# Two transformer blocks on one core: other duration estimates for side work, NSA compression in column quarters, 512-column feed-forward tails and memory values, small weights loaded first

## Chip, core and metric

The kernel runs on one core of a Trainium2 chip, as one program. The metric is the time of one execution in microseconds; lower is better. TensorE (PE) multiplies matrices, VectorE (DVE), ScalarE (ACT) and GpSimd (POOL) work on elements, SyncE (SP) issues most of the DMAs.

## What is computed

Two blocks of two layers each, on a sequence of 256 rows of 1024 elements. The first block's layer is a mixer (an LRU, "forgetting" attention with 8 heads, and retention with 4 heads), cross attention to a memory of 256 rows, and a gated feed-forward. The second block's layer is a feed-forward, a mixer of three attentions (NSA with a compressed, a selected and a window branch; stick-breaking; sliding window), and a second feed-forward. Cut to what the change touches:

```python
def swiglu(h, w_gate, w_up, w_down):              # six times in all
    return (jax.nn.silu(h @ w_gate) * (h @ w_up)) @ w_down

def memory_cross_attention(h, mem_n, w_q, w_k, w_v, w_o):
    k = (mem_n @ w_k).reshape(bsz, m, CROSS_HEADS, CROSS_HEAD_DIM)
    v = (mem_n @ w_v).reshape(bsz, m, CROSS_HEADS, CROSS_HEAD_DIM)
    ...

def compress(t, w1, w2):                           # in nsa_attention, for keys and for values
    blocks = t[:, cmp_idx] + cmp_pos[:, None, :]   # 15 overlapping blocks of 32 rows, 2 groups
    blocks = blocks.transpose(0, 3, 1, 2, 4).reshape(B, G, n_cmp, CMP_LEN * Dh)
    return jax.nn.silu(blocks @ w1) @ w2           # w1: 2048 x 256, w2: 256 x 64
```

## The kernel before

**Big products.** Every large matrix product is made of three FP32R products (hi x hi, hi x lo, lo x hi) of operands split into two parts. Weights come from HBM as raw chunks of 1 MB (class `Weights`, three raw buffers); ScalarE casts a piece to `whi`, VectorE subtracts to get `wlo`, up to six pieces ahead of TensorE. Activations are kept transposed and split (`thi`, `tlo`; `mhi`, `mlo` for the memory). Products gather in PSUM tiles `acc`, two of them in a ring. A raw chunk is freed, and the next load issued on SP, when its last piece is split. Feed-forward weights are taken in column blocks of 512 and one tail of 256: the gate's block, then the up block (`ffn`, `plan_ffn`). `gate_done` applies silu on ScalarE, `up_done` multiplies on VectorE.

**Side work.** Attention, the LRU, retention, the norms and the NSA compression are Python generators handed to `side()`. At fixed points between the big products the writer calls `pump()`. There, class `Pace` keeps an estimated clock for each engine while the program is written: each instruction adds an estimated duration, a tile's estimated time of being ready is kept, and a step of a side generator is put into the instruction streams once its inputs are estimated ready (0.3 us of slack) and a bank of the two `aux` PSUM tiles is free. Where the writer needs a result that isn't there yet, `finish()` or `pump(force=True)` puts the missing steps in one behind the other, with no big products between. The order in which instructions stand in each engine's stream is fixed by this at build time; on the chip an engine waits where an input is late. Small products write `aux`, `o0` and `o1`. All instructions are recorded by one helper, so the trace gives line 150 for nearly everything; groups are told apart by tile names.

**Names.** `sc`, `pt`, `fv`, `fkT`, `fqT`, `fT`: forgetting attention. `rot`, `rqkT`, `rvg`, `cv`, `bd`: retention and its rotary step (`h`: the LRU's output or a norm's row). `cqT`: cross attention. `kvout`: the memory's keys and values on their way to HBM (`fill_steps`). In the second mixer (`mixer2`): `rs`, `wkT`, `wqT`, `wv` sliding window; `rn`, `kT`, `qT`, `vsw` the selected and window branches of NSA, in eight units (transposes of `rn`, scores `kT,qT`, softmax, values `rn,vsw`); `kc`, `kcb`, `scmp`, `pc` the compressed branch; `w`, `hh`, `hv` its second weights and hidden rows.

**NSA compression.** `compress_blocks` lays out the blocks, splits them in two parts (`t`), and `compress_mm` multiplies them with the split weight: 30 output rows, 256 columns, three products per 128 rows of the weight, 96 per layer, between the branch gate's big products (`compress_mm` is called between weight pieces as planned by `plan_mixer2`). `compress_attention` turns the 30 rows by four transposes and loads the second weights and masks just before it uses them.

Of the kernel before, what the change touches and what calls it, by code (L numbers as in the profile page):

```python
# [48 lines left out]
class Pace:  # L49
# [3 lines left out]
    FIXED = {"vector": (0.065, 1.045e-3), "scalar": (0.075, 0.86e-3), "gpsimd": (0.13, 2.15e-3)}  # L53
# [3 lines left out]
    def __init__(self, nc):  # L57
# [3 lines left out]
        self.loads = 0.0  # L61
        for name in ("tensor", "vector", "scalar", "gpsimd", "sync"):
            self.at[name] = 0.0
            setattr(self, name, Paced(self, name, getattr(nc, name)))
# [22 lines left out]
    def op(self, name, op, args, kwargs):  # L87
# [15 lines left out]
        elif name == "tensor":  # L103
            moving = aps[2] if op == "matmul" else aps[0]
            rate = 1 if moving.dtype == F32R else 2 if op == "transpose" else 4
            self.products = start + max(0.027, size(moving) * rate / 2400.0) + 0.004
            done = self.products + 0.1
        else:
            fixed, each = self.FIXED[name]
            n = max(size(a) for a in aps)  # L110
            if kwargs.get("op") == ALU.pow:
                fixed, each = 0.3, 0.165
# [5 lines left out]
            self.at[name] = max(start, self.at[name]) + (fixed + each * n) + (0.09 if kwargs.get("accum_out") is not None else 0.0)  # L118
            done = self.at[name] + 0.1
# [35 lines left out]
class Weights:  # L155
# [10 lines left out]
    def plan(self, ap, c0, c1, k0, k1, a_chunk, a_piece, split=True, gain=None, halves=0):  # L166
# [4 lines left out]
        for k in range(k0, k1, a_chunk):  # L171
# [6 lines left out]
            self.chunks.append((parts, a, b))  # L178
            for j in range(0, a, a_piece):
                n = min(a_piece, a - j)  # L180
                self.pieces.append([ci, j, n, b, split, j + n >= a, None, list(range(k + j, k + j + n)), gain])
# [7 lines left out]
    def _load(self):  # L189
# [5 lines left out]
        for ps, ap in parts:  # L195
            self.nc.sync.dma_start(v[ps], ap)
# [72 lines left out]
def tile_two_blocks(ctx, tc, I, out):  # L269
# [52 lines left out]
    def mm(ps, a, b, start, stop):  # L322
        nc.tensor.matmul(ps, a, b, start=start, stop=stop)

# [11 lines left out]
    def pump(force=False):  # L336
# [33 lines left out]
    def two_aux():  # L370

        while max([nc.idle(a) for a in auxs[-2:]], default=0.0) > nc.products + 0.3:
# [31 lines left out]
    def pair_scores(q, k):  # L404

        pss = aux(), aux()
        for c, qs, ks in ((slice(0, P), slice(0, P), slice(0, P)), (slice(P, 384), slice(P, S), slice(0, S))):
            for u in (0, 1):
                mm(pss[u][:, c], q[HALF[u], qs], k[HALF[u], ks], start=True, stop=True)
        return pss  # L410

    def pair_scores_T(q, k):

        pss = aux(), aux()
        for c, ks, qs in ((slice(0, S), slice(0, P), slice(0, S)), (slice(S, 384), slice(P, S), slice(P, S))):
            for u in (0, 1):
                mm(pss[u][:, c], k[HALF[u], ks], q[HALF[u], qs], start=True, stop=True)
# [20 lines left out]
    def pair_pv(dst, ws, vs, start=True, stop=True):  # L438

        for kt, (c0, c1, q0) in enumerate(((0, S, 0), (S, 384, P))):  # L440
            for u in (0, 1):
                mm(dst[HALF[u], q0:S], vs[u][:, kt, :], ws[u][:, c0:c1], start=start and kt == 0, stop=stop and kt == 1)
# [330 lines left out]
    def plan_ffn(g, u, d, gain):  # L773
        for c0, c1 in FBLOCKS:
            for w in (g, u):
# [1261 lines left out]
```

## Time and profile before

| what | us |
|---|---|
| median of three runs (lowest, highest) | 2108.08 (2105.86, 2108.32) |
| the profiled execution | 2107.61 |
| its span in the trace | 2105.8 |
| TensorE busy | 2053.1 |
| VectorE busy | 1276.0 |
| ScalarE busy | 1120.7 |

The profiled execution lies between the three runs. TensorE's busy time overstates its work somewhat, because consecutive products overlap in the trace and their ends are modelled; the distance from start to start is the better measure of what one costs. In the views below "x" is a count, and what stands in square brackets or behind the bar is the idle time before an instruction and what ended it. PEclk is TensorE's granted clock as a share of full speed.

### The profile page before, as it was taken

The page shows a single profiled execution, that of the slowest core. Times are in us where ns is not written, and L with a number is a line of the kernel's source. Part 1 is how long each engine was busy: PE and PEld are TensorE (multiplying, and loading weights), DVE is VectorE, ACT ScalarE, POOL GpSimd, SP SyncE. Part 2 cuts the span into 40 slices and gives each one's busy share as a digit, 9 for nine tenths or more (in the row PEclk, how much of TensorE's full clock was granted, in tenths as well). Part 3 has the DMA queues.
Part 4 walks back from the last instruction along what each step waited for, and adds up shares of the span by engine and source line. Part 5 has one row for each costly group of instructions (what it writes and reads, how often), then busy time and mean ns, then how long its engine had stood idle before and what let it go on. Part 6 is the DMA issues. An engine that isn't in the chain of part 4 may idle for free.

```text
span 2105.8 us, 28507 instructions
## 1 busy us (share of the span) xinstructions
PE 2053.1 (97%) x10982; PEld 1717.3 (82%) x10982; DVE 1276.0 (61%) x2187; ACT 1120.7 (53%) x1910; POOL 84.7 (4%) x110
## 2 busy tenths in 40 slices
PE   7999999999899999999999999999999999999999
PEld 6889888888797788788888767888888887768887
DVE  6766566556664755655467666664655567756553
ACT  5556566455465654555355655554555456446552
POOL 0210000002100000000001000000000001000000
PEclk9999999999999999999999999999999999999999
DMA  7555565654465565555646544555555547545553
GB/s 244 182 194 190 186 212 180 212 178 158 148 225 175 182 198 191 172 187 180 210 145 207 169 140 158 193 176 193 180 196 194 162 151 230 144 132 183 179 197 103
DMA packets 204583, 380.86 MB, mean 181 GB/s; under 512 B 14160, under 2 KB 78464, under 8 KB 204448
## 3 DMA queue, kind: packets, MB, share of 16 engines
q1 hardware_dynamic: 192928, 366.46, 53.1%
q10 hardware_dynamic: 11520, 12.59, 2.0%
q8 instruction: 86, 1.41, 0.3%
q14 instruction: 49, 0.40, 0.1%
HBM read 372.03 MB, written 6.99 MB: 180 GB/s over the span
## 4 chain that ended last, share of the span: by engine, by line
PE 83%; DVE 6%; ACT 4%; DMA 4%; issue 2%; POOL 0%; SPq 0%; ACTq 0%; DVEq 0%; POOLq 0%
PE acc L150 74%; PE aux L150 6%; DVE wlo L150 3%; PE o L150 3%; ACT whi L150 1%; DMA nb<-cdram 1%; DMA raw<-in_w_in_dram 1%; DMA w<-in_nsa_cmp_k_w_dram 1%; ACT rn L150 1%; ACT thi L150 1%; DMA kvd<-kvout 0%; SPq L150 0%; DVE t L150 0%; DVE h L150 0%; DMA mem<-in_mem_dram 0%
## 5 line engine op out<-in xcount | busy, mean ns | idle before, releaser
L150 PE MATMUL acc<-whi,thi 128*128 128x512 f32 (+2 forms) x1856 | 716.2, 386 | 2.3 <-ACT thi L150 1.4
L150 PE MATMUL acc<-whi,tlo 128*128 128x512 f32 (+2 forms) x1856 | 699.9, 377 | 2.5 <-DVE tlo L150 2.4
L150 PE MATMUL acc<-wlo,thi 128*128 128x512 f32 (+2 forms) x1856 | 699.3, 377 | 3.1 <-DVE wlo L150 2.8
L150 DVE TENSOR_TENSOR wlo<-raw,whi 128x1024 fp32r<-128x1024 f32 (+1 forms) x386 | 463.0, 1210 | 310.1 <-ACT whi L150 308.3
L150 ACT CAST whi<-raw 128x1024 fp32r<-128x1024 f32 (+1 forms) x386 | 393.7, 1037 | 243.9 <-PE acc L150 219.9
L150 DVE SCALAR_TENSOR_TENSOR wlo<-raw,prm,whi 128x512 fp32r<-128x512 f32 (+1 forms) x640 | 398.5, 680 | 173.8 <-ACT whi L150 173.6
L150 ACT ACTIVATE whi<-raw,prm 128x512 fp32r<-128x512 f32 (+1 forms) x640 | 379.9, 663 | 90.2 <-PE acc L150 86.7
L150 PEld LDWEIGHTS acc<-whi,thi 128*128 128x128 f32 x1856 | 350.3, 189 | 72.4 <-issue 9.3
L150 PEld LDWEIGHTS acc<-whi,tlo 128*128 128x128 f32 x1856 | 349.9, 189 | 70.3 <-DVE tlo L150 6.4
L150 PEld LDWEIGHTS acc<-wlo,thi 128*128 128x128 f32 x1856 | 350.5, 189 | 64.4 <-DVE wlo L150 6.1
L150 PE MATMUL acc<-whi,ahi 128*128 128x512 f32 x528 | 206.9, 392 | 0.0
L150 PE MATMUL acc<-whi,alo 128*128 128x512 f32 x528 | 205.7, 389 | 0.0
L150 PE MATMUL acc<-wlo,ahi 128*128 128x512 f32 x528 | 205.6, 389 | 0.0
L150 PEld LDWEIGHTS acc<-whi,alo 128*128 128x128 f32 x528 | 99.1, 188 | 20.8
L150 PEld LDWEIGHTS acc<-whi,ahi 128*128 128x128 f32 x528 | 99.2, 188 | 19.9
L150 PEld LDWEIGHTS acc<-wlo,ahi 128*128 128x128 f32 x528 | 99.2, 188 | 19.9
L150 POOL TENSOR_TENSOR r<-v,mhalf 128x1 f32<-128x1 f32 (+3 forms) x46 | 48.1, 1047 | 1593.9 <-DVE v L150 1591.9
L150 PE MATMUL acc<-thi,whi 128*128 128x256 f32 x384 | 111.9, 291 | 0.0
L150 PE MATMUL acc<-tlo,whi 128*128 128x256 f32 x384 | 108.6, 283 | 0.0
L150 PE MATMUL acc<-thi,wlo 128*128 128x256 f32 x384 | 108.5, 283 | 0.0
L150 DVE SCALAR_TENSOR_TENSOR silu<-acc,r,silu 128x512 f32<-128x512 f32 (+1 forms) x72 | 47.5, 702 | 100.4 <-PE acc L150 100.4
L150 ACT CAST ahi<-aux 128x512 fp32r<-128x512 f32 (+1 forms) x72 | 39.8, 553 | 121.9 <-PE aux L150 121.7
(301 smaller groups left out, 1946.9 us busy)
## 6 DMA issues: line engine op xcount, KB each, us to landing
raw<-in_w_in_dram SPq DMA_DIRECT2D x65, 1024.0 KB, 5.1
raw<-in_ffn_w_gate_dram SPq DMA_DIRECT2D x44, 1024.0 KB, 5.1
raw<-in_ffn_w_up_dram SPq DMA_DIRECT2D x44, 1024.0 KB, 5.1
raw<-in_ffn_w_down_dram SPq DMA_DIRECT2D x44, 1024.0 KB, 4.9
raw<-in_w_gate_dram SPq DMA_DIRECT2D x22, 1024.0 KB, 5.0
raw<-in_w_up_dram SPq DMA_DIRECT2D x22, 1024.0 KB, 5.1
raw<-in_w_down_dram SPq DMA_DIRECT2D x22, 1024.0 KB, 4.8
raw<-in_w_out_dram SPq DMA_DIRECT2D x16, 1024.0 KB, 5.0
```

The lines of the kernel that those rows point to most:

```text
L150: return f(*args, **kwargs)
```

## The change

Five edits in one. (1) The estimates of `Pace` are other numbers, mostly longer, and the 0.3 us of slack in `pump` and `two_aux` is gone; the second of two products in opposite halves of the array counts as 7 ns. (2) The compression uses unsplit fp32 blocks and raw weights: four products of 32 output rows and 256 columns stand side by side, each in its own quarter of the array's columns, 32 per layer; the four partial sums are added by a product with `sel` (the identity folded four times), which takes the place of the transposes. The raw chunk is freed when TensorE is done with it. (3) The feed-forward tails of gate and up stand side by side as one block of 512 columns; silu and the product both follow its end. (4) The memory's value weights are taken in 512-column blocks, and `kvout` is written once per pair. (5) `load_small` issues the DMAs of the compression's second weights and masks when `compress_blocks` begins. Also: `xs` has one buffer, the sliding window waits for `blocks` where it waited for the split blocks, and the forgetting attention waits for a flag that its decay rows are on their way to HBM.

```diff
-    FIXED = {"vector": (0.065, 1.045e-3), "scalar": (0.075, 0.86e-3), "gpsimd": (0.13, 2.15e-3)}
+    FIXED = {"vector": (0.15, 1.06e-3), "scalar": (0.14, 0.89e-3), "gpsimd": (0.25, 3.3e-3)}
...
-            rate = 1 if moving.dtype == F32R else 2 if op == "transpose" else 4
-            self.products = start + max(0.027, size(moving) * rate / 2400.0) + 0.004
-            done = self.products + 0.1
+            main = moving.dtype == F32R
+            if op == "transpose":
+                took = 0.109
+            elif self.beside:
+                took = 0.007
+            elif main:
+                took = (size(moving) + 32) / 2400.0
+            else:
+                took = max(0.224, size(moving) * 4 / 2400.0)
+            self.products = start + took + (0.09 if main != self.main else 0.0)
+            self.main = main
+            done = self.products + 0.25
...
-            due = [i for i in ready if i[1] <= nc.products + 0.3 and aux_free() <= nc.products + 0.3]
+            due = [i for i in ready if i[1] <= nc.products and aux_free() <= nc.products]
...
-                W.plan(I[f"nsa_cmp_{kv}_w1_2"][l], 0, 256, 8 * k, 8 * k + 8, 8, 4)
+                W.plan(I[f"nsa_cmp_{kv}_w1_2"][l], 0, 256, 8 * k, 8 * k + 8, 8, 4, split=False)
...
-                            mm3(a[:30, k * S : k * S + S], bh[:, k, kt, :], bl[:, k, kt, :], hi[:, j, :], lo[:, j, :], kt == 0, kt == 15)
+                            mm(a[32 * j : 32 * j + 32, k * S : k * S + S], blocks[:, k, kt, :], w[:, j, :], i == 0, i == 3, beside=j > 0)
...
-                        turn(ps[:, (2 * k + b) * 30 : (2 * k + b + 1) * 30], raw[:, k * S + b * P : k * S + (b + 1) * P], ident[:30, :30])
+                        mm(ps[:, (2 * k + b) * 30 : (2 * k + b + 1) * 30], raw[:, k * S + b * P : k * S + (b + 1) * P], sel[:, :30], start=True, stop=True)
...
-            for w in (g, u):
-                W.plan(w, c0, c1, 0, 8, 4 if c1 - c0 == 512 else 8, 2 if c1 - c0 == 512 else 4, gain=gain)
+            if c1 - c0 == 512:
+                for w in (g, u):
+                    W.plan(w, c0, c1, 0, 8, 4, 2, gain=gain)
+            else:
+                W.plan(g, c0, c1, 0, 8, 4, 2, gain=gain, beside=u)
...
+                    if n < 512:
+                        hold["n"] = n
+                        gate_done(a)
...
+            W.plan(I["w_cv"][l], c // 2 * 512, c // 2 * 512 + 512, 4 * (c % 2), 4 * (c % 2) + 4, 4, 2)
...
+                        if kind == "v":
+                            mm3(a[:, b * 512 : b * 512 + 512], MT.hi[:, kt, bs], MT.lo[:, kt, bs], hi[:, j, :], lo[:, j, :], kt == 0, kt == 7)
...
-                    xs = mp.tile([P, 16, 32], F32, tag="xs", name=nm("xs"))
+                    xs = mp.tile([P, 16, 32], F32, tag="xs", name=nm("xs"), bufs=1)
...
             def compress_blocks():
+                load_small()
```

How TensorE's stream moves is shown at two places of the second mixer in layer 0. The first is where the sliding window, the compressed branch and one NSA unit stand. Before, on PE, with twelve or six big products (`acc`) between the steps:

```order
L150 MATMUL aux_10735<-w_856_10666,hh_10645 30x64 x2
L150 MATMUL aux_10735<-w_857_10667,hv_862_10679 128x64 x2
L150 MATMUL o_10655<-rs_10725,wv_9544 64x256
...
L150 MATMUL acc_10569<-whi_10535,thi_9111 128x512
...
L150 MATMUL aux_10780<-ident_90,kc_10743 128x30
L150 MATMUL acc_10784<-whi_10553,thi_9111 128x512
...
L150 MATMUL aux_10809<-kcb_10782,qT_9546 128x30 x8
L150 MATMUL acc_10784<-whi_10605,thi_9111 128x512
...
L150 MATMUL aux_10835<-ident_90,rn_10695 128x128 x3
```

With the change, on PE, the same steps:

```order
L163 MATMUL aux_10356<-w_781_9645,hh_10289 30x64 x2
L163 MATMUL aux_10356<-w_782_9646,hv_854_10315 128x64 x2
L163 MATMUL o_10378<-rs_10327,wv_9147 64x256
...
L163 MATMUL aux_10383<-ident_90,kc_10364 128x30
L163 MATMUL aux_10387<-kcb_10385,qT_9149 128x30 x8
L163 MATMUL aux_10403<-ident_90,rn_10208 128x128 x3
...
L163 MATMUL aux_10429<-kT_9150,qT_9149 128x128
...
L163 MATMUL aux_10447<-ident_90,pc_10417 128x128 x2
```

No `acc` product stands between them any more; the row without big products runs from the second transposes of `rs` to the transposes of the next unit's `rn`, thirteen steps.

The second place is the end of the same mixer, before the last rows of the NSA branch are needed. Before, on PE, from the last big product on:

```order
L150 MATMUL acc_11333<-whi_11194,tlo_9542 128x512
L150 MATMUL o_11262<-rn_11287,vsw_9545 64x256
...
L150 MATMUL aux_11357<-ident_90,rn_11309 128x128 x3
...
L150 MATMUL aux_11369<-kT_9547,qT_9546 128x128
...
L150 MATMUL o_11262<-rn_11365,vsw_9545 64x256
...
L150 MATMUL aux_11397<-ident_90,rn_11377 128x128 x3
...
L150 MATMUL o_11262<-rn_11405,vsw_9545 64x256
```

With the change, on PE, from the last big product on:

```order
L163 MATMUL acc_10760<-whi_10664,tlo_9145 128x512
L163 MATMUL aux_10774<-ident_90,rn_10682 128x128 x3
...
L163 MATMUL o_10814<-rn_10782,vsw_9148 64x256
...
L163 MATMUL aux_10819<-ident_90,rn_10798 128x128 x3
...
L163 MATMUL o_10814<-rn_10827,vsw_9148 64x256
...
L163 MATMUL aux_10863<-ident_90,rn_10843 128x128 x3
...
L163 MATMUL o_10814<-rn_10871,vsw_9148 64x256
...
L163 MATMUL aux_10903<-ident_90,rn_10883 128x128 x3
```

Two sets of `rn` transposes follow the last big product before, and four with the change.

## Rows read from the trace of the kernel before

**Rows 1.** The page, busy time of each engine:

```profile
PE 2053.1 (97%) x10982; PEld 1717.3 (82%) x10982; DVE 1276.0 (61%) x2187; ACT 1120.7 (53%) x1910; POOL 84.7 (4%) x110
```

**Rows 2.** The page, the chain of work that ended last, by engine:

```profile
PE 83%; DVE 6%; ACT 4%; DMA 4%; issue 2%; POOL 0%; SPq 0%; ACTq 0%; DVEq 0%; POOLq 0%
```

**Rows 3.** Windows by stage: length, then each engine's busy us, clock, DMA:

```profile
core 0: us, PE busy (x) PEld busy (x) DVE busy (x) ACT busy (x) POOL busy (x), PEclk, DMA share, GB/s
0.00:184.00 184.00, 169.37 (x1134) 149.30 (x1135) 123.09 (x250) 103.11 (x185) 26.25 (x40) 0.99 0.60 197
...
452.00:640.00 188.00, 180.35 (x1203) 159.78 (x1202) 120.82 (x227) 103.22 (x191) 21.28 (x31) 0.97 0.57 187
...
1067.00:1267.00 200.00, 191.70 (x1112) 152.26 (x1113) 131.35 (x290) 110.81 (x214) 10.48 (x6) 0.99 0.55 169
1267.00:1680.00 413.00, 412.23 (x1974) 344.36 (x1974) 242.67 (x339) 216.06 (x335) 4.30 (x7) 1.00 0.55 182
```

**Rows 4.** Waits of PE: us in total, times, the longest:

```profile
PE aux L150 <- DVE rn L150: 6.0, 4, 2.1
PE aux L150 <- DMA w<-in_nsa_cmp_k_w_dram: 3.8, 2, 2.6
PE aux L150 <- DVE rs L150: 2.9, 2, 1.5
...
PE aux L150 <- ACT cqT L150: 2.4, 2, 1.2
...
PE o L150 <- DVE rvg L150: 2.2, 1, 2.2
PE aux L150 <- DVE sc L150: 2.0, 1, 2.0
PE aux L150 <- DVE fT L150: 1.9, 1, 1.9
PE acc L150 <- ACT kvout L150: 1.9, 1, 1.9
PE aux L150 <- DVE rot L150: 1.7, 2, 1.5
...
PE aux L150 <- ACT pt L150: 1.1, 1, 1.1
```

**Rows 5.** Timeline of PE (start, duration): a 512-column stretch, a feed-forward tail:

```profile
1131.13 0.40 PE L150 MATMUL acc<-wlo,thi 128*128 128x512 f32 x1
...
1135.44 0.39 PE L150 MATMUL acc<-whi,tlo 128*128 128x512 f32 x1
...
992.18 0.28 PE L150 MATMUL acc<-wlo,thi 128*128 128x256 f32 x1
...
1000.56 0.28 PE L150 MATMUL acc<-whi,tlo 128*128 128x256 f32 x1
```

**Rows 6.** Timeline of PE in the compression, a stretch's third and last product:

```profile
1136.70 0.42 PE L150 MATMUL o<-whi,t 128*30 128x256 f32 x2 [0.64 <-DVE t L150]
...
1139.14 0.28 PE L150 MATMUL o<-whi,t 128*30 128x256 f32 x1
```

**Rows 7.** Timeline of PE: fp32 side products, whole and in halves:

```profile
94.69 1.02 PE L150 MATMUL aux<-cv,bd 128*128 128x256 f32 x4
95.65 0.87 PE L150 MATMUL o<-pt,fv 128*64 128x256 f32 x8
96.45 0.50 PE L150 MATMUL acc<-whi,thi 128*128 128x512 f32 x1
```

**Rows 8.** Windows: the stretch behind the wait for sc (columns as rows 3):

```profile
77.15:80.56 3.41, 3.41 (x12) 2.71 (x11) 3.30 (x8) 0.96 (x2) 0.10 (x1) 0.53 0.43 137
```

**Rows 9.** Timeline of PE, end of the second mixer in layer 0:

```profile
1255.79 1.16 PE L150 MATMUL aux<-ident,rn 128*128 128x128 f32 x6 [0.98 <-DVE rn L150]
...
1261.35 1.44 PE L150 MATMUL aux<-ident,rn 128*128 128x128 f32 x6 [2.06 <-DVE rn L150]
...
1266.84 0.50 PE L150 MATMUL acc<-whi,thi 128*128 128x512 f32 x1 [0.68 <-ACT thi L150]
```

**Rows 10.** Groups by form, ScalarE: silu of a feed-forward tail (busy, mean ns):

```profile
L150 ACT ACTIVATE silu<-acc,r 128x256 f32<-128x256 f32 x12 | 5.0, 471 | 13.7 <-PE acc L150 13.7
```

More of the change, by code (lines that the diff above doesn't have):

```diff
@@ L117, in op @@
                     self.at[name] = max(start, self.at[name]) + 1.3
-            self.at[name] = max(start, self.at[name]) + (fixed + each * n) + (0.09 if kwargs.get("accum_out") is not None else 0.0)
-            done = self.at[name] + 0.1
+            if name == "scalar" and op == "activation":
+                fixed, each = 0.3, 0.8e-3
+            self.at[name] = max(start, self.at[name]) + (fixed + each * n) + (0.19 if kwargs.get("accum_out") is not None else 0.0)
+            done = self.at[name] + 0.15
         for a in [out, kwargs.get("accum_out")]:
@@ L164, in __init__, with plan @@
         self.limit = None
-    def plan(self, ap, c0, c1, k0, k1, a_chunk, a_piece, split=True, gain=None, halves=0):
+    def plan(self, ap, c0, c1, k0, k1, a_chunk, a_piece, split=True, gain=None, halves=0, beside=None):
         b = c1 - c0
@@ L177, in plan @@
                 parts = [(slice(0, P), ap[k * P : (k + a) * P, c0:c1].rearrange("(a p) n -> p a n", p=P))]
-            self.chunks.append((parts, a, b))
+            parts = [(ps, slice(0, b), v_) for ps, v_ in parts]
+            if beside is not None:
+                parts.append((slice(0, P), slice(b, 2 * b), beside[k * P : (k + a) * P, c0:c1].rearrange("(a p) n -> p a n", p=P)))
+            self.chunks.append((parts, a, b * (1 if beside is None else 2)))
             for j in range(0, a, a_piece):
                 n = min(a_piece, a - j)
-                self.pieces.append([ci, j, n, b, split, j + n >= a, None, list(range(k + j, k + j + n)), gain])
+                self.pieces.append([ci, j, n, b * (1 if beside is None else 2), split, j + n >= a, None, list(range(k + j, k + j + n)), gain])
     def start(self, n):
@@ L320, in tile_two_blocks, with mm @@
     sides = []
-    def mm(ps, a, b, start, stop):
+    def mm(ps, a, b, start, stop, beside=False):
+        nc.beside = beside
         nc.tensor.matmul(ps, a, b, start=start, stop=stop)
+        nc.beside = False
     def turn(ps, src, by):
@@ L370, in two_aux @@
     def two_aux():
-        while max([nc.idle(a) for a in auxs[-2:]], default=0.0) > nc.products + 0.3:
+        while max([nc.idle(a) for a in auxs[-2:]], default=0.0) > nc.products:
             yield max(nc.idle(a) for a in auxs[-2:])
@@ L408, in pair_scores @@
             for u in (0, 1):
[L409 removed]
+                mm(pss[u][:, c], q[HALF[u], qs], k[HALF[u], ks], True, True, beside=u > 0)
         return pss
@@ L441, in pair_pv @@
             for u in (0, 1):
-                mm(dst[HALF[u], q0:S], vs[u][:, kt, :], ws[u][:, c0:c1], start=start and kt == 0, stop=stop and kt == 1)
+                mm(dst[HALF[u], q0:S], vs[u][:, kt, :], ws[u][:, c0:c1], start and kt == 0, stop and kt == 1, beside=u > 0)
     def put_T(T, kt0, ob):
@@ L983, in out_ @@
                         put_T(M, 1 + b, ob[0])
+                while "cdram" not in flags:
+                    yield False
                 load_nb(0)
@@ L1472, in swa @@
             def swa():
-                while "wqk_ready" not in hold or "blocks_ready" not in hold:
+                while "wqk_ready" not in hold or "blocks" not in hold:
                     yield False
@@ L1727, in compress_attention @@
             def compress_attention(a):
-                raw = t2()[:30]
-                nc.scalar.copy(raw, a[:30])
+                raw = t2()
+                nc.scalar.copy(raw, a)
+                sel = one([P, 32], "sel")
+                nc.vector.tensor_reduce(sel, ident.rearrange("p (j m) -> p m j", j=4), axis=AX.X, op=ALU.add)
                 hold["cmp"] = True
```

72 lines of the change are left out of this document (42 added, 30 removed).

## The prediction

> **What bounds the kernel now.** I read the page first: TensorE is busy 97% of the span [rows 1], and the chain that ended last is 83% TensorE, 6% VectorE, 4% ScalarE and 4% DMA [rows 2]. So a change can win in two ways only: fewer or shorter products, or less of the time in which TensorE stands still. The table by stage shows where it stands still: the two long feed-forward stretches are nearly full, and the gaps lie in the four mixers, 15 us in the first (the start of the program included), 8 us in the second, 8 us in the first NSA mixer and as much in its twin of layer 1 [rows 3]. (A busy TensorE is overstated in this table, since the modelled end of one product overlaps the next. By starts against the usual pitch I get 8.8, 9.4, 11.8 and 13.6 us of waits.) The list of waits names their causes [rows 4]: rn and rs (softmax rows), w (a small weight), fT, sc, rvg, rot and kvout. A gap of some 2 us costs more than itself: after the 1.96 us wait for sc the next 3.41 us ran at a granted clock of 0.53, half speed [rows 8], which loses another 1.6 us. The profiled execution took 2107.61 us (span 2105.8), 0.5 us under the median of 2108.08; the sum is made against it and 0.5 us added at the end.
>
> **Fewer products.** Three edits take work off TensorE, all of it on the path.
> Tails: the 256-column products of a feed-forward tail start 0.120 us apart (992.18 to 1000.56, 70 steps) and 512-column ones 0.227 us apart (1131.13 to 1135.44, 19 steps) [rows 5]. Six times 96 products become 48: 6 x (96 x 0.120 - 48 x 0.227) = 3.7 us gained. Memory values: 384 products become 192, 384 x 0.120 - 192 x 0.227 = 2.5 us.
> Compression: 192 products for both layers, 0.116 us apart (21 steps, 1136.70 to 1139.14), with 1.3 us of waits for t beside them [rows 6]: 23.6 us. In its place stand 64 fp32 products of 256 columns, four to a group, each in its own quarter of the columns. The trace shows no quarters. It shows what one fp32 product of 256 columns costs alone: two in a row took from 94.69 to 95.65, 0.48 us each. And it shows halves: eight instructions, which are two products of 256 and two of 128 columns in both passes, took 0.80 us, where by the former rate they would need some 1.4 [rows 7]. So halves run beside each other. If quarters do too, 16 groups x 0.45 (0.48 less a share for the change of kind) = 7.2 us; if only two run at once 14.4; if none, 64 x 0.45 = 28.8. I take the first, as the halves are the nearest rows: 16.4 us gained; the ends are 9 us gained and 5 us lost. The Trainium skill (TensorE: Matmul & The Clock Gate, section on packing small matmuls) gives three column tiles a measured 2.38 times, not three; by an estimate from it a group would take 0.45 x 3 / 2.38 = 0.57 us and the gain be 14.5 instead of 16.4 us. No run here shows three or four tiles.
> The sixteen fewer splits of 1024 elements on ScalarE and VectorE are hidden, since these engines are not the bound; that a raw chunk now stays taken until TensorE is done costs nothing as long as one 1 MB load with its split lands within the products of the chunk between (24 x 0.227 = 5.4 us and the next burst), with a margin under 1 us; if it is missed, the price is that part of a us at four places a layer.
> Work in all: -3.7 - 2.5 - 16.4 = -22.6 us.
>
> **Later side steps.** With longer estimates a step of attention goes into TensorE's stream later, so fewer steps meet unready inputs; but what has not been placed when its result is needed comes in one row with no big products between. So waits go at the spots of [rows 4] and come at the forced stretches. The price of a forced stretch can be read, because the end of each NSA mixer is one already: its softmax units follow each other from 1255.79 to 1261.35, 5.56 us each, of which transposes (0.65), scores and values (some 0.8 each, as in [rows 7]) are about 2.2 us of TensorE and the rest waits (one of 2.06 us); the tail, from 1261.35 to the next big product at 1266.84, takes 5.5 [rows 9]. Amid big products the same unit costs its 2.2 us and, by an estimate from the starts around such bursts, three changes between the two kinds at some 0.2 us.
> *End of the NSA mixers.* Two further units of each layer move into the forced end: 2 x (5.56 - 2.2 - 0.6) = 5.5 us a layer, and about 1.5 us more a layer for the half clock that follows gaps of 2 us [rows 8]: +14 us for both layers.
> *First stretch of the NSA mixers.* The branch merge needs the sliding-window result, and thirteen steps (sliding window, compressed attention, one unit) now stand in one row, where before they lie between big products. TensorE's own work in the row is about 10 us, an estimate at the rates of [rows 7, 9]. The handovers, estimates too, between: some four of a PSUM copy (0.6 us each), two waits for a bank (0.5), the norm of the compressed keys (1.7), its softmax (2.5), and the splitting of the result (1.3, less 0.8 hidden): 9 us, with one drop of the clock, 1.6. Against it: eleven bursts less, 2.2, and the waits for rs, w and the transposed t of before, 3.1 and 4.4 us in the two layers with a clock drop of 1.6 in the second. 10.6 - 5.3 = +5.3 and 10.6 - 8.2 = +2.4: +7.7 us. The bounds: 6 us of waits if ScalarE and VectorE have run ahead, 18 if each handover costs as much as the 2.06 us.
> The small weights' earlier load is in this: it takes the 3.8 us wait for w away [rows 4], but the same step stands in the forced row, behind hh. Six more issues on SP ahead of one 1 MB load are hidden by the pieces already split.
> *First mixer, layer 0.* Gone: fT 1.9, sc 2.0 with its half clock 1.6, and pt 1.1 [rows 4, 8], nine bursts 2.0: 8.6. New: a forced row of eight steps before the memory fills (two PSUM copies, two decay products, one norm, and the split of the memory behind it, about 7.7 us) and the last two units of the forgetting attention, 3.7: +2.8 us net, from 0 to +9.
> *First mixer, layer 1.* Gone: rot 2.0, rvg 2.2, kvout 1.9 [rows 4] and three stretches at half clock, 5.0; new: the same forced end, 3.7: -7.4 us. *Cross attention*: -1.5 us, two waits for cqT.
> *Tails again.* silu and the product now both follow the block's end, 2 x 0.47 + 0.48 us in a chain [rows 10], while the next block has its first accumulator free for 6 to 12 products (1.4 to 2.7 us): 0 to 0.5 us, I take 0.3 x 6 = +1.8. Two loads per chunk in place of one: hidden. xs with one buffer makes VectorE wait for GpSimd about 1.5 us twice, hidden by the five pieces split ahead.
> Waits in all: 14 + 7.7 + 2.8 - 7.4 - 1.5 + 1.8 = +17.4 us.
>
> **The sum.** 2107.6 - 22.6 + 17.4 + 0.5 = 2103 us, 0.24% faster.
>
> **Rivals.**
> *A. The forced rows cost little.* ScalarE and VectorE are busy 53% and 61% [rows 1]; they may have worked ahead on the steps that are only late on TensorE. Then the first stretch is +1 and not +7.7, the end +8 and not +14, the first mixer 0, the silu 0: 2087 us. Against it: the exposed units of [rows 9] had the same engines free and yet took 5.56 us.
> *B. Slower: the first forced row of the NSA mixers is a single chain.* With two PSUM banks for side work every one of its ten handovers may wait like rn, about 1.8 us and not 0.9: 18 us a layer and not 9: +18, 2121 us. It decides from about 1.4 us a handover on, where the time passes 2112. For it: the waits for rn and rs in the list, 1.5 to 2.1 us at the longest; against it: half the handovers are mere copies.
> *C. The quarters do not run beside each other.* 28.8 and not 7.2 us: 2124 us. Against it the halves of [rows 7]; for it that no row shows quarters, and that fp32 takes two passes.
> *D. The estimates don't do what they say*: the list of waits of after would name the same rs, sc, rot; the work terms alone would then be left, 2086 us. I count it with A.
>
> **How the numbers follow.** About 0.2% (4.2 us) is what a measurement of this kernel can tell from no change. Forecast (2095 to 2110): 0.42, of which 0.22 below 2103.9, 0.14 within 0.2% and 0.06 above. A and D: 0.26, faster. B: 0.22 and C: 0.10, slower. So faster 0.48, same 0.14, slower 0.38. The range runs from A to B and C and leaves out the outer part of each: 2087 to 2123.
>
> **What would show it.** Right: groups of four quarter products with starts a few ns apart and a group every 0.45 us; no wait for sc, rot, rvg, kvout or fT in the list, and in their place rn, rs, kc and pc; TensorE standing still some 20 us in each NSA mixer, in a row without big products; their stages longer by some 3 us even after 8 us less compression each. Wrong: NSA stages shorter than before (A), first rows of over 25 us (B), o<-raw products that start 0.2 us or more apart within a group (C), or gaps among the big products of the feed-forward stretches, where I expect none over 0.5 us.

## The result, and the profile after

The changed kernel took 2163.71 us in the median (2160.09 to 2163.81, four runs), the kernel before beside it 2108.2. The ratio is 1.0255, 95% interval 1.0233 to 1.0278: slower by 55 us where 5 us faster was forecast, and 41 us above the upper end of the range. The profiled execution has a span of 2162.0 us.

The page of after, busy time of each engine and the chain that ended last, to be held against [rows 1, 2]:

```profile
PE 2070.4 (96%) x10446; PEld 1700.5 (79%) x10446; DVE 1256.1 (58%) x2123; ACT 1098.5 (51%) x1842; POOL 88.9 (4%) x112
...
PE 84%; DVE 5%; ACT 4%; DMA 4%; issue 2%; POOL 0%; ACTq 0%; SPq 0%; DVEq 0%; POOLq 0%
```

These two rows hardly tell that anything is wrong. VectorE and ScalarE have less to do, as the change meant, and TensorE seems busier by 17 us although it has 536 matmul instructions fewer. The clock column (PEclk) of the table by stage tells why: at a lower granted clock the same products are busy for longer. The stages are cut here at the first transposes of x in the kernel's stages (windows of after, columns as [rows 3]: length, PE busy, ..., PEclk, DMA share, GB/s):

```profile
0.00:188.30 188.30, 164.10 (x989) 139.12 (x990) 116.09 (x231) 97.39 (x165) 25.70 (x38) 0.96 0.57 185
...
264.40:621.10 356.70, 341.73 (x1805) 286.36 (x1804) 210.40 (x330) 181.57 (x291) 22.56 (x34) 0.97 0.53 177
...
888.70:1333.40 444.70, 425.38 (x2111) 339.56 (x2110) 259.58 (x465) 219.84 (x381) 13.10 (x13) 0.96 0.52 169
1333.40:1521.00 187.60, 187.03 (x854) 154.48 (x853) 107.12 (x144) 98.28 (x148) 1.54 (x2) 1.00 0.56 185
1521.00:1968.20 447.20, 424.80 (x2110) 340.43 (x2109) 256.79 (x459) 217.76 (x377) 12.59 (x12) 0.95 0.51 166
```

The same cuts in the trace of before, and for every step of TensorE its distance to the next start, sorted into the usual pitch of such a product (work), what half speed added (clock), what followed a semaphore (waits) and the rest:

| stage | before, us | after, us | forecast difference | measured difference |
|---|---|---|---|---|
| first mixer, layer 0 | 174.0 | 188.3 | +1.5 | +14.3 |
| feed-forward, then first mixer, layer 1 | 349.3 | 356.7 | -9 | +7.4 |
| cross attention, both | 155.9 | 153.1 | -1.5 | -2.8 |
| feed-forward and NSA mixer, layer 0 | 428.5 | 444.7 | +3.8 | +16.2 |
| feed-forward and NSA mixer, layer 1 | 427.3 | 447.2 | +0.9 | +19.9 |
| the other three feed-forwards | 570.6 | 572.0 | -0.9 | +1.4 |

Over the whole kernel, with the prediction's own terms sorted in the same way (the wait for t, which it counted with the compression, stands with the waits):

| | before, us | after, us | forecast difference | measured difference |
|---|---|---|---|---|
| work at the usual pitch | 1993.3 | 1973.2 | -21.3 | -20.1 |
| waits | 53.0 | 97.2 | +26.9 | +44.2 |
| clock | 8.1 | 36.9 | -2.0 | +28.8 |
| rest (changes between the kinds of product) | 38.2 | 41.7 | -8.8 | +3.5 |

So the products were saved, and 77 us came in elsewhere, nearly all of it in the four mixers, where 16 were forecast. Clock and waits can't simply be added as causes: while a chain runs at half speed its waits are shorter.

The waits of PE in after (us in total, times, longest), beside [rows 4]:

```profile
PE aux L163 <- DVE sc L163: 11.9, 2, 8.4
...
PE aux L163 <- DVE wng L163: 9.3, 4, 4.1
PE aux L163 <- DVE rn L163: 8.9, 6, 2.1
PE aux L163 <- DVE kk L163: 6.7, 2, 3.4
PE acc L163 <- ACT thi L163: 6.3, 7, 2.8
PE aux L163 <- DVE rot L163: 6.1, 4, 4.0
```

As forecast, fT, rvg, kvout and w are gone. What was not forecast: sc and rot are larger than before, and kk and wng are new.

The clock is in the windows over the rows without big products (after, columns as above):

```profile
88.90:105.10 16.20, 10.64 (x67) 9.01 (x65) 9.26 (x19) 3.17 (x7) 0.00 (x0) 0.89 0.47 140
583.90:599.40 15.50, 5.60 (x29) 3.26 (x27) 8.27 (x23) 7.84 (x18) 2.89 (x3) 0.63 0.20 77
1217.50:1241.90 24.40, 18.41 (x93) 13.09 (x92) 14.17 (x58) 7.78 (x28) 0.79 (x2) 0.65 0.20 63
1277.80:1302.20 24.40, 19.23 (x87) 11.83 (x85) 8.84 (x43) 9.70 (x33) 0.00 (x0) 0.65 0.07 22
```

In the last two rows the DMAs are busy 0.20 and 0.07 of the time, where the stages above have 0.51 to 0.57, and ScalarE 8 to 10 of 24.4 us: for 24 us a chain of small steps runs and little else. The clock records show half speed for 115 us in all, against 23 before (113 and 21 of it within the span), in stretches of up to 17.07 us; I had counted one of 3.41 us for each row.

The end of the NSA mixer in layer 0, PE, beside [rows 9] and two more lines of the same unit there (before, then after):

```profile
1257.06 1.43 PE L150 MATMUL aux<-kT,qT 64*128 64x128 f32 x8
1258.42 0.87 PE L150 MATMUL o<-rn,vsw 128*64 128x256 f32 x8
```

```profile
1283.52 1.42 PE L163 MATMUL aux<-ident,rn 128*128 128x128 f32 x6 [2.06 <-DVE rn L163]
1284.87 2.34 PE L163 MATMUL aux<-kT,qT 64*128 64x128 f32 x8
1287.14 1.55 PE L163 MATMUL o<-rn,vsw 128*64 128x256 f32 x8
1289.95 1.59 PE L163 MATMUL aux<-ident,rn 128*128 128x128 f32 x6 [1.26 <-DVE rn L163]
...
1302.46 0.50 PE L163 MATMUL acc<-whi,thi 128*128 128x512 f32 x1 [0.68 <-ACT thi L163]
```

Here the forecast held: four units and the tail take 24.4 us, a unit 6.4 where [rows 9] had 5.56. The scores (kT,qT) take 2.34 us where they took 1.43. The values (rn,vsw) take 1.55 where they took 0.87, but the wait for rn behind them is shorter by about as much, 1.26 for 2.06.

### The profile page after: what moved, and what is told of

Same layout as the page of the kernel before. It is cut to its first block, busy times and chain, and to the rows that moved or that the text cites. A ratio compares the mean times of both kernels' runs of the same rounds, so it can differ in the third digit from the quotient of the medians.

```text
span 2162.0 us, 27301 instructions
## 1 busy us (share of the span) xinstructions
PE 2070.4 (96%) x10446; PEld 1700.5 (79%) x10446; DVE 1256.1 (58%) x2123; ACT 1098.5 (51%) x1842; POOL 88.9 (4%) x112
## 4 chain that ended last, share of the span: by engine, by line
PE 84%; DVE 5%; ACT 4%; DMA 4%; issue 2%; POOL 0%; ACTq 0%; SPq 0%; DVEq 0%; POOLq 0%
PE acc L163 75%; PE aux L163 7%; PE o L163 2%; DVE wlo L163 2%; ACT whi L163 2%; DMA raw<-in_w_in_dram 1%; ACT rn L163 1%; DMA nb<-cdram 1%; ACT thi L163 1%; DMA kvd<-kvout 1%; DMA bt<-btiles 0%; DVE rs L163 0%; DVE h L163 0%; DVE rn L163 0%; DVE tlo L163 0%
## 5 line engine op out<-in xcount | busy, mean ns | idle before, releaser
L163 PE MATMUL acc<-whi,thi 128*128 128x512 f32 (+1 forms) x1760 | 701.1, 398 | 8.7 <-ACT thi L163 6.3
L163 PE MATMUL acc<-whi,tlo 128*128 128x512 f32 (+1 forms) x1760 | 686.6, 390 | 4.4 <-DVE tlo L163 4.3
L163 PE MATMUL acc<-wlo,thi 128*128 128x512 f32 (+1 forms) x1760 | 685.5, 390 | 3.8 <-DVE wlo L163 3.6
L163 DVE TENSOR_TENSOR wlo<-raw,whi 128x1024 fp32r<-128x1024 f32 (+1 forms) x370 | 443.5, 1213 | 306.8 <-ACT whi L163 306.0
L163 ACT CAST whi<-raw 128x1024 fp32r<-128x1024 f32 (+1 forms) x370 | 377.3, 1037 | 275.7 <-PE acc L163 223.8
L163 ACT ACTIVATE whi<-raw,prm 128x512 fp32r<-128x512 f32 (+1 forms) x592 | 371.7, 694 | 103.7 <-PE acc L163 100.2
L163 PEld LDWEIGHTS acc<-whi,thi 128*128 128x128 f32 x1760 | 334.0, 190 | 84.2 <-ACT thi L163 9.4
L163 PEld LDWEIGHTS acc<-whi,tlo 128*128 128x128 f32 x1760 | 333.2, 189 | 78.8 <-DVE tlo L163 10.5
L163 PEld LDWEIGHTS acc<-wlo,thi 128*128 128x128 f32 x1760 | 333.9, 190 | 70.3 <-DVE wlo L163 6.8
L163 ACT ACTIVATE silu<-acc,r 128x512 f32<-128x512 f32 (+1 forms) x72 | 43.1, 650 | 114.6 <-PE acc L163 114.6
```

The source lines that it names most:

```text
L163: return f(*args, **kwargs)
```

## Experiments

In what follows P is the theory that the new estimates and the places they give to the side steps make the loss, and O that the other edits do. All ratios are to the kernel before on the same chip; its medians there were 2108 to 2110 us.

**The estimates against the rest.** First the changed kernel without edit 1:

```diff
-    FIXED = {"vector": (0.15, 1.06e-3), "scalar": (0.14, 0.89e-3), "gpsimd": (0.25, 3.3e-3)}
+    FIXED = {"vector": (0.065, 1.045e-3), "scalar": (0.075, 0.86e-3), "gpsimd": (0.13, 2.15e-3)}
...
-            due = [i for i in ready if i[1] <= nc.products and aux_free() <= nc.products]
+            due = [i for i in ready if i[1] <= nc.products + 0.3 and aux_free() <= nc.products + 0.3]
```

> The changed kernel with edit 1 undone: the old durations in Pace and the 0.3 us of slack in pump and two_aux; compression in quarters, 512-column tails and memory values and the early small weights stay. Theory P (placement): everything that was lost, 44 us of waits and 29 us of half clock, comes from where the new estimates put the side steps; then the 20 us of work that the other edits save show up whole: 2083 to 2095 us, half clock under 30 us in all. Rival O (the other edits): the raw compression chunks held by TensorE and the doubled buffers block ScalarE (the wait for kk, 3.5 us in each layer) and lose most of it: 2110 us or more.

Measured: 2129.34 us, ratio 1.009 (1.0061 to 1.0118). Then the reverse, the kernel before with edit 1 alone:

> The kernel before with edit 1 alone: new durations and no slack. Theory P: the waits and the half clock of the changed kernel without its savings: 2165 to 2185 us, half clock 80 to 120 us. Rival O: under 2130 us.

Measured: 2163.79 us, ratio 1.0261 (1.0227 to 1.0295), 1 us below theory P's window. Both theories are half right. Edit 1 costs 54 us by itself, all of the loss. But the other edits are no gain either: with the old estimates they save 24 us of TensorE's work and still come out 20 us slower. The two losses don't add: together they make 55 us, not 74.

**Durations, TensorE's costs, slack.** Edit 1 was taken apart. The slack of 0.3 us put back into the changed kernel:

> The changed kernel with only the 0.3 us of slack in pump and two_aux put back; the new durations stay. If the durations drive the steps into the forced rows: 2145 to 2165 us, forced rows of the NSA mixers still over 20 us. If the missing slack does: 2100 to 2130 us.

Measured: 2176.55 us, ratio 1.0312 (1.0281 to 1.0344), slower still and above both expectations. The first row of the NSA mixer fell apart into two (14.9 and 17.8 us), the end stayed at 24.3. So putting the slack back does not bring the loss back down. What its absence does with the old durations was not tried by itself.

The kernel before with only the longer durations of VectorE, ScalarE and GpSimd (and the flag on the decay rows, which this order of steps needs):

> The kernel before with only the element engines' part of edit 1: the longer durations of VectorE, ScalarE and GpSimd; TensorE's costs and the 0.3 us of slack as before. If these durations make the rows without big products (54 small products at the end of each NSA mixer, as in the changed kernel, where the kernel before has 30): 2145 to 2165 us, near the 2164 of all new estimates. If TensorE's costs and the slack do it: under 2125 us.

Measured: 2167.31 us, ratio 1.0266 (1.0251 to 1.0282): all of edit 1's loss, from a handful of numbers that no engine ever executes. The other half of edit 1 (TensorE's costs together with the missing slack), and the durations half way:

> The kernel before with the other half of edit 1: the new costs of TensorE's instructions and no slack, the old durations of the element engines. Its last rows have 40 small products, the first 20. If the loss follows the rows: 2115 to 2132 us. If these parts are harmless: 2104 to 2112 us.

Measured: 2129.48 us, ratio 1.0087 (1.0066 to 1.0108).

> The kernel before with durations of VectorE, ScalarE and GpSimd half way between the old and the new numbers; all else as before. Its last row of each NSA mixer has 48 small products (30 before, 54 with the new ones), the first 26 (none of that length before, 41). If the loss follows the rows: 2128 to 2148 us. If any shift costs the same: 2155 us or more. If only the full length does harm: under 2120 us.

Measured: 2153.78 us, ratio 1.0201 (1.0176 to 1.0226), 6 us above its window; the end of the mixer had its 48 small products and took 23.4 us. Half the shift of the numbers made three quarters of the loss. Against the length of all stretches of over 4 us without a big product (from the starts in each trace, the compression's products counted as big), the kernels with other estimates rise together:

| kernel | such stretches, us | span, us |
|---|---|---|
| before | 53 | 2105.8 |
| TensorE's costs and no slack | 80 | 2127.1 |
| half durations | 121 | 2153.6 |
| new durations alone | 148 | 2164.4 |
| all of edit 1 | 150 | 2162.5 |

Against before, each us of such a stretch costs 0.6 to 0.8 us. (The rest of it is the stretch's own small products, which must run somewhere.) The changed kernel has 170 us of them, and with its 20 us less work it fits as well. So the loss grows with what is moved out of the cover of big products. It is not all: the kernel with the small weights loaded early, below, has 46 us of such stretches, less than before, and is slower all the same. So a rival stays in part: the old numbers may sit at a good point by chance, where small shifts lose too. No run took shorter durations.

**The clock.** To part the price of the half clock from that of the waiting, TensorE was given something to do while it waits: ahead of a forced step's own products, products of the identity with itself go into the bank that these overwrite, as many as fill a share of the wait that Pace foresees.

```diff
+        for _ in range(min(40, int(0.7 * gap[0] / 0.23))):
+            nc.nc.tensor.matmul(t[:, :P], ident, ident, start=True, stop=True)
...
+                gap[0] += max(nc.products, i[1], aux_free()) - nc.products
                 nc.products = max(nc.products, i[1], aux_free())
```

> The changed kernel, with products of the identity with itself put ahead of a forced step's own products, into the PSUM bank that these overwrite: as many as fill 0.7 of the wait that Pace foresees (0.22 us each). TensorE then hardly stands still in the forced rows, and nothing else changes. If the half clock there is a price of its own, about 29 us: half clock under 60 us instead of 115, and 2135 to 2148 us. If the forced rows are set by VectorE and ScalarE anyhow, and the clock only goes along with it: 2158 us or more.

Measured: 2172.73 us, ratio 1.0289 (1.0254 to 1.0325). The mean granted clock was 0.995, as in the kernel before, and half speed lasted 25 us in all: the expectation on the clock came true. By its number the time is that of the second case, but it does not decide between them, because the added products made rows longer themselves: at full clock from end to end the first row of the NSA mixer in layer 0 took 28.2 us and its end row 24.7, where both took 24.4. I take it that too many of the added products stood on the chain. With 0.3 in the place of 0.7:

> The changed kernel with products of the identity with itself in the forced gaps as before, but for 0.3 of each foreseen wait and not 0.7. If the half clock has a price of its own (some 1 us for each of the exposed units of 6.5 us, where at full clock they took 5.56): half clock under 70 us, 2150 to 2158 us. If the rows are set by the element engines alone: 2160 us or more.

Measured: 2163.83 us, ratio 1.0249 (1.0219 to 1.0279), the time of the changed kernel; half speed lasted 76 us, 6 more than the first case allows. In the end row, at full clock from end to end, PE shows (busy_gaps_less; line 319 is the added products):

```profile
1295.28 1.16 PE L163 MATMUL aux<-ident,rn 128*128 128x128 f32 x6 [0.74 <-DVE rn L163]
1296.55 0.49 PE L319 MATMUL aux<-ident 128*128 128x128 f32 x2
1296.96 1.02 PE L163 MATMUL aux<-kT,qT 64*128 64x128 f32 x8
1297.91 0.87 PE L163 MATMUL o<-rn,vsw 128*64 128x256 f32 x8
1298.71 1.60 PE L319 MATMUL aux<-ident 128*128 128x128 f32 x12
1300.97 1.16 PE L163 MATMUL aux<-ident,rn 128*128 128x128 f32 x6 [0.65 <-DVE rn L163]
```

A unit takes 5.69 us (1295.28 to 1300.97), as good as the 5.56 of [rows 9], and the row 21.5 us instead of 24.4. The end row of layer 1 is 21.5 us too. So half speed did cost there, but 2.9 us of the 8.5 that 17 us at half speed make by the clock alone: where VectorE and ScalarE have a share of the chain, only the small products on it get longer. The first rows took the gain back. They grew from 24.4 and 22.9 to 30.9 and 26.2 us, and in layer 0 half speed did not go: it lasted 23.9 us at a stretch, longer than in the changed kernel. The clock is a minor part of the loss in the end rows, which show it cleanly; for the others its share stays open.

**The other edits, one at a time, each on the kernel before with the old estimates.**

> The kernel before with the feed-forward tails as one block of 512 columns alone. Work: 3.7 us less by starts (96 x 0.120 against 48 x 0.227, six times); the silu behind the block's end gives back up to 2 us and a split piece that is late 0.7 us at each feed-forward (the wait for whi in the changed kernel). 2104 to 2109 us; 2104.5 if only the work counts, 2108 if the two cancel.

Measured: 2107.45 us, ratio 0.9996 (0.9986 to 1.0006). The starts save their 0.6 to 0.7 us at each feed-forward, and each gives as much back in waits and changes of kind: the three feed-forwards that stand alone take 190.2, 187.3 and 193.2 us, where they took 190.2, 187.2 and 193.2. The changed kernel has a wait of 0.57 us for whi at each. The cancelling that was named there is what happened.

> The kernel before with the memory values in 512-column pieces alone (with the doubled kvout tile and xs in one buffer). Work: 2 to 2.5 us less. Theory V: the pair's one late copy of kvout and its one DMA make cross attention wait (cpr and hk, about 4 us more in each cross stage with the old estimates): 2110 to 2118 us. Rival: no new waits, 2105 to 2107 us.

Measured: 2115.17 us, ratio 1.0034 (1.0021 to 1.0047). Both cross stages grew by 4 us, as theory V says, but kvout is not the reason. The transposes of the last head's probabilities, in this kernel and in the kernel before (PE timelines of values_alone, then of before):

```profile
227.88 0.83 PE L150 MATMUL aux<-ident,cpr 128*128 128x128 f32 x4 [3.01 <-DVE cpr L150]
```

```profile
228.39 0.70 PE L150 MATMUL aux<-ident,cpr 128*128 128x128 f32 x4 [0.17 <-DVE cpr L150]
```

The softmax ends within about half a us of the same time in both. Before, big products lay over it; here none are left, and TensorE waits for 3.0 us in the open and then runs at half speed for 3.41. One layer later it waits 3.4 us for hk, which SP began to load at 652.12, long after the last write of kvout was issued at 617.13. Why that load is late was not followed.

> The kernel before with the compression's small weights and masks loaded at the start of compress_blocks alone. The waits for w go (1.3 and 2.6 us, the second with 1.7 us of half clock). 2103 to 2106 us if they were all that was late there; 2108 if the step then waits for hh or kc instead.

Measured: 2116.17 us, ratio 1.0034 (1.0022 to 1.0046): neither. The waits for w are gone, but the NSA stages are longer by 5.0 and 3.6 us. Their new waits are (waits of PE, small_alone):

```profile
PE o L150 <- DVE t L150: 3.6, 2, 1.8
PE o L150 <- ACT t L150: 3.6, 2, 1.8
```

Counted from the start of the stage, TensorE comes to the compression at the same time as before, but the split of the blocks (t) is 2.4 us later: in ScalarE's stream two weight casts and a square more stand ahead of it. I had called six issues on SP hidden, and on SP they are; but each issue also moves Pace's clock, and with it the order on other engines. That this is the whole mechanism was not shown.

> The kernel before with the compression in column quarters alone (raw unsplit weights, the product with sel; old estimates, a quarter counting 7 ns; small weights loaded late). Its products save 15 us of TensorE's work. Theory H (the held chunk): the raw chunk is freed only when TensorE is done with it, the load after it is issued that late, ScalarE stands before its cast for 5 us twice in each layer and everything behind it in its queue is late: about 14 us of new waits and half clock in each of the two NSA mixers, so 2110 to 2122 us. Rival N (the quarters are harmless, the loss in the kernel with the old estimates comes from elsewhere): 2090 to 2097 us.

Measured: 2117.89 us, ratio 1.0047 (1.0029 to 1.0066), within theory H. The groups are as forecast: each product is two instructions, the four of a group start 7 ns apart, and a group takes 0.432 us (0.456 for the first of a burst). A chunk's burst of two groups, from one big product's place to the next, takes 1.09 us, 8.7 us for all eight where 7.2 were counted. But ScalarE's casts show where the gain went. Groups by form, ScalarE, of before, of the changed kernel and of the experiment with the copied chunk, below (busy, mean ns, idle before and by whom):

```profile
L150 ACT CAST whi<-raw 128x1024 fp32r<-128x1024 f32 x376 | 388.6, 1049 | 243.9 <-PE acc L150 219.9 <-DVE rot L150 9.4 <-DMA raw<-in_w_in_dram 6.9
```

```profile
L163 ACT CAST whi<-raw 128x1024 fp32r<-128x1024 f32 x360 | 372.0, 1050 | 275.7 <-PE acc L163 223.8 <-DMA raw<-in_w_in_dram 41.7 <-issue 5.3
```

```profile
L163 ACT CAST whi<-raw 128x1024 fp32r<-128x1024 f32 x360 | 372.2, 1049 | 247.4 <-PE acc L163 223.6 <-DMA raw<-in_w_in_dram 13.6 <-issue 5.3
```

The number behind raw<-in_w_in_dram tells it: ScalarE waited 41.7 us for raw loads of the input projection, where it was 6.9. At 1157.13 SP issues the load of the next big chunk, just as TensorE ends the burst that held the buffer; ScalarE stands before its cast until 1162.17; kk is behind it in ScalarE's and VectorE's queues (timelines of after: SP, ACT, PE):

```profile
1157.13 0.38 SPq L163 DMA_DIRECT2D raw<-in_w_in_dram  x1
```

```profile
1162.17 1.05 ACT L163 CAST whi<-raw 128x1024 fp32r<-128x1024 f32 x1 [6.10 <-DMA raw<-in_w_in_dram]
```

```profile
1167.44 0.63 PE L163 MATMUL aux<-ident,kk 128*128 128x128 f32 x4 [3.30 <-DVE kk L163]
```

**Taking the held chunk away.** The raw chunk is copied, half by ScalarE and half by VectorE, into the two buffers of one split piece, and is free as early as before:

```diff
+                if split == "copy":
+                    flat = raw.rearrange("p a n -> p (a n)")
+                    nc.scalar.copy(hi.bitcast(F32), flat[:, :PIECE])
+                    nc.vector.tensor_copy(lo.bitcast(F32), flat[:, PIECE:])
```

> The changed kernel, but a raw compression chunk is copied, half by ScalarE and half by VectorE, into the two buffers of a split piece (1.05 us each in place of nothing), so that the raw buffer comes free early and loads run ahead as in the kernel before. Theory H (the held chunk makes ScalarE stand before its next cast): the waits for kk, 3.5 us in each layer, and the half clock behind them (1.7 us each) go; the rows without big products stay. 2148 to 2156 us. Rival (kk is late for another reason): 2160 to 2167 us.

Measured: 2161.82 us, ratio 1.0249 (1.0233 to 1.0264). The wait for the loads fell to 13.6 us and the wait for kk is gone, so the mechanism is shown; the time is the rival's. In this kernel waits for nngm (2.1), t (1.8 and 2.5), nsum (1.9 in each layer) and a longer one for kcb (3.5 where it was 1.1) took its place in the same stages.

> The kernel with the old estimates and all other edits, with the copied chunk as above. Theory H: the waits for ta, wng and rs of that kernel (about 13 us over both layers, and the half clock behind them) go: 2108 to 2118 us, with what values and small weights lost alone still in it. Rival: the steps move again and something else in these mixers is late: 2122 us or more.

Measured: 2118.74 us, ratio 1.004 (1.0026 to 1.0053), 10.6 us less than with the held chunk, and 0.7 us above theory H's window. With the old estimates the cause was worth its price; with the new ones the chain behind it was late anyway.

**The best of the parts.**

> The kernel before with only the two edits that were not slower by themselves or should not be with the copied chunk: 512-column tails, and quarters with the copied chunk; old estimates, memory values and small weights as before. Work 3.7 and 15 us less, 64 copies of about 1 us beside it in the place of 64 splits of 2.3 us. 2086 to 2096 us if no new wait comes; 2100 us or more if the moved steps of the NSA mixers run into new ones.

Measured: 2107.91 us against 2109.74, ratio 0.999 (0.998 to 0.9999). Some 19 us of work are gone and 2 us are won. In the two NSA stages the time is what it was (428.2 for 428.5, and 426.7 for 427.3 us): waits for wng (2.8 and 2.9), wes (1.3 in each layer) and sel (1.0 in each layer) have come in, where TensorE now arrives before the softmax. Earlier steps, by 0.6 us of slack instead of 0.3, were tried on it:

> The kernel before with 512-column tails and quarters with the copied chunk, and the slack in pump and two_aux at 0.6 us in place of 0.3, so that steps go earlier. If lateness is what costs, earlier steps cost less in the rows and more among the big products: 2098 to 2106 us. If the old estimates already sit near the best point: 2108 us or more.

Measured: 2120.05 us, ratio 1.0053 (1.0034 to 1.0072); the first mixer of layer 0 alone grew by 10 us, and in each NSA mixer TensorE came so early that it waited 6.3 us for the small weights (w). The best version is 2 us in 2110 faster than the kernel before, and its interval ends just under 1; all others are slower or the same.

## Why the prediction was wrong

**The saved work** was right: 21.3 us forecast without the wait for t, 20.1 by the starts. Quarters run beside each other, so rival C falls. The term was 1.5 us too good (8.7 us for the 7.2 forecast), for what each burst costs at its ends; within a group the trace shows four at the time of one. By an estimate from the Trainium skill's 2.38 times (TensorE: Matmul & The Clock Gate, section on packing small matmuls) the sixteen groups would take 9.1 us. The measured total is near that, but not group by group: in the changed kernel none took more than 0.456 us, where the estimate has 0.57.

**The places and the exposed unit** were right in the NSA mixers. Four units at the end were priced from [rows 9], and took 24.4 us; the waits of the two stages rose by 10.1 and 13.4 us, where the terms of the sum give some 12 and 11. The waits named as gone (fT, pt, rvg, kvout, w) did go. The handovers of the first row, as listed, add up to some 8 us and not to the 9 in the sum, and rival A's terms to 2086 and not 2087; neither changes the picture.

**The term that is furthest off is the clock**: "with one drop of the clock, 1.6". I took from [rows 8] that a gap of 2 us brings 3.41 us at half speed, and counted one for a row, against three stretches that went. In a row of such gaps half speed goes on: up to 17.07 us, 115 us over the kernel. By the clock alone that is 31 us more than forecast. Not all of that is time lost. The end rows of the NSA mixers, each with 17.07 us at half speed, took 24.4 us, and the forecast's own terms make 23.7 (three units of 5.56, the tail of 5.5, and 1.5 for the clock): the waits in the row shrank as the products grew. Filled with products, the same row says that a third of the clock's sum lies on the path (2.9 of 8.5 us). How much the others would win at full speed is not settled, because the products that kept the clock up also lengthened their chains.

**By place** the four rows forecast in the NSA mixers came out 7.5 us too long together, 24.4 and 22.9 us for 20.6 at the first and 24.4 for 23.7 at the ends. The stages missed their forecasts by 62 us: 29 in the first mixers (with the feed-forward ahead of the second), 31 in the NSA stages. So most of it lies where the forecast had no row, or put too little on one; the steps below are these. In the NSA mixer of layer 1, two waits for wng (4.1 and 1.4 us) in a row of 7.3 us had no term at all.

**The second is the covers.** "Eleven bursts less, 2.2" a layer, and the like elsewhere, was -8.8 us; the rest rose by 3.5. Steps that stand behind each other save fewer changes than I counted; no run shows why. And "hidden" was said of the small weights' six issues and of the one buffer of xs, and the paired kvout got no term; alone the two edits cost 8 and 7 us. Values is the plain case: it saves 2.5 us of products, and a softmax loses its cover. In the changed kernel that loss does not show, since its cross stages are 2.8 us shorter; what the small weights cost there was not tried.

**The third is the exposed end of the first mixers**, "the last two units of the forgetting attention, 3.7". I priced it from the exposed unit of another attention, [rows 9], which had all its transfers issued by 1248, before its exposed units began. The trace of after, PE:

```profile
593.73 1.59 PE L163 MATMUL aux<-ident,sc 128*128 128x128 f32 x6 [8.38 <-DVE sc L163]
```

These 8.38 us are one step with all its inputs in the open: the decay rows are fetched by a DMA issued on ScalarE's queue only at 584.31, GpSimd masks them at 587.65, then comes the softmax on VectorE and ScalarE, and in VectorE's queue a split, a norm's sum and a product of the retention stand before its last scaling. In layer 0 it was 3.5, with 2.0 us for tlo some time before it. There the row before the memory fills adds a wait of 4.05 us for rot. Together the waits of the first mixers were 16 us above the terms.

**The fourth** is "costs nothing as long as one 1 MB load with its split lands within the products of the chunk between". It did not land in time (issued at 1157.13, it let the cast begin at 1162.17), and I had taken TensorE for the only one to wait: ScalarE waits in its queue, and all side work behind it does. That was 10.6 us with the old estimates, and two waits for kk of 3.3 us and more in the changed kernel, with half speed for 3.41 us behind each, where taking them away only showed the next late step.

**The rivals.** A and D fall: sc and rot are still in the list, but at other places. B had the right sign and a place that counted, at less than its price: the first rows took 24.4 and 22.9 us, where the forecast's terms make 20.6 and B's about 30. Slower had a chance of 0.38, but no case reached beyond 2124 us, because each was the forecast with one term changed, while the clock, the covers and the first mixers were short in the same direction.

## What to carry to other kernels

Where side work is placed at build time by estimated readiness, an estimate that is nearer to the truth need not be the better one. Here the new ones are nearer: a 512-element product on VectorE took 0.68 us in the trace of before, where the old estimate makes 0.60 and the new one 0.69. A step placed late is pushed to the point where its result is needed, and there its whole chain stands in the open: here some 0.6 us for each us of row without big products. Earlier is not free either: with 0.6 us of slack on the old estimates the best version lost 12 us. Price such an edit by counting these rows in the new order over the whole program, not at two chosen places.

Saving products that lie over a dependent chain need not save time: 19 us less work moved this kernel by 2 us. And a buffer that is freed by a later engine must be followed to the engine that issues the next load and to the one that waits for it, with everything queued behind.

## What the chip showed unexpectedly

Four fp32 products of 32 output rows and 256 columns in the four column quarters start 7 ns apart and take 0.432 us together, the time of one (mk,cqT in the trace of before: two instructions 0.216 us apart); each burst of two such groups costs another 0.2 us at its ends. Half speed stayed for up to 17.07 us at a time in the changed kernel while short products with gaps of 1 to 2 us between them ran. With small fp32 products put into the gaps it did not come at all in a row of 21.5 us, but in another row of the same kernel it lasted 23.9. The unit of the chain then took 5.69 us, against 6.4 to 6.5 at half speed: the clock's price on a chain set by other engines was 0.8 us in 6.5.
